# A two-layer decoder in split float32: token-major products in two of 256 columns, weights of theirs 128 bytes further on, other products gathered, and wide runs behind them

## The chip, the core and the metric

The kernel runs on one core of a Trainium2 chip. The metric is the device time of one execution in microseconds, as the median of the runs. In the profile PE is TensorE's matmul stream and PEld its weight loads, DVE is VectorE, ACT is ScalarE, POOL is GpSimd and SP is SyncE.

## What is computed

The input `x` has 256 tokens of 2,048 features. There are two layers. The first has a gated MLP that mixes tokens within chunks of 128, the second has attention with 16 heads and forget gates. Each ends with a feed-forward part (2,048 to 2 x 5,632, a causal convolution of width 3, SiLU gate, back to 2,048). The reference, cut to what matters:

```
def chunked_gmlp(xn, w_in, v_norm, w_s, b_s, w_out):
    z = gelu(xn @ w_in)
    u, v = split(z, 2)
    v = rmsnorm(v, v_norm)
    mixed = einsum('gts,bnsgc->bntgc', tril(w_s), v) + b_s
    return (u * mixed) @ w_out

def conv_ffn(xn, w_up, conv_w, conv_b, w_down):
    h = xn @ w_up
    h = sum(shift(h, k) * conv_w[k] for k in range(3)) + conv_b
    gate, val = split(h, 2)
    return (silu(gate) * val) @ w_down

h = x + chunked_gmlp(rmsnorm(x), ...)
h = h + conv_ffn(rmsnorm(h), ...)
k, v, c = keys, values, cumulative log forget gates of rmsnorm(h) @ w_kvf
h = h + forgetting_attention(rmsnorm(h), ..., k, v, c)
h = h + conv_ffn(rmsnorm(h), ...)
return rmsnorm(h)
```

All weights are float32, 418 MB of them are read once.

## The kernel before

**The products.** A float32 product is made of three in the type float32r. Each weight chunk is split into a rounded part `whi` (ACT, line 82) and the remainder `wlo` (DVE, line 83). The activations are kept as a rounded half and a remainder half side by side: `X1[:, kt, :256]` and `X1[:, kt, 256:]` (and `X2`, `H` in the same form). Needed are whi times both halves and wlo times the rounded half.

**The stream.** `Stream` (lines 40 to 102) runs a list of weight chunks of 128 x 1,024 numbers, 512 KB each, in order. At step i it loads chunk i + 6 (SP's queue), splits chunk i + 3 (ACT and DVE), multiplies chunk i (`mult`), and then advances every pending generator by one `yield`. The generators are what follows a block of chunks: evictions, norms, the convolution, the heads. So the instructions of such a step stand on every engine's queue behind the products of one chunk and ahead of those of the next. There are four buffers of each of `raw`, `whi` and `wlo`.

**Two orientations.** `feat_block` (line 168) makes two rows of 128 output features for all tokens: the weights are the stationary operand, the activations stream. A chunk has eight pieces of weights. Normally a piece of whi takes two products of 256 columns, one for each half of the activations, into the same 256 columns of the accumulator, and a piece of wlo takes one: 24 narrow products. Where the chunk's number is in `wide`, whi takes both halves in one product of 512 columns. Then the halves land side by side in the accumulator and have to be added afterwards (`both`, lines 309 to 316 and 323). `wide` is all four chunks for the first up block of a feed-forward part and for the gates `b_g`, the second chunk for the blocks of u, and the first chunk of some other blocks.

`tok_block` (line 214) makes 512 output features for two blocks of 128 tokens: the activations are loaded as the stationary operand, the weights stream, always 512 columns at a time, 12 products a chunk. It is used for v of the MLP, for q, k and v of the attention.

**Other products on TensorE.** They stand in generators between two chunks: mixing (line 489, one pair of groups behind each block of u), token sums and their transposes (350, 290), transposes of the normalised q and k (575, one for each token block), and for each head the scores (660, 661), the transposes of the probabilities (676) and the products with v (683 to 685), as three separate steps. These work on plain float32.

**Accumulators.** PSUM holds three double accumulators `ps` for the blocks (`main_ps`) and two single ones `mp` for the other products (`misc_ps`).

Of the kernel before, what the change touches and what calls it, by code (L numbers as in the profile page):

```python
# [17 lines left out]
P = 128  # L18
# [10 lines left out]
LOADS = 6  # L29
NEG = -3e38  # L30
# [9 lines left out]
class Stream:  # L40
# [7 lines left out]
    def chunk(self, src, mult, at_load=None, at_split=None):  # L48
        self.items.append((src, mult, at_load, at_split))

    def then(self, at_load=None, at_split=None, at_mult=None):
        self.items.append((None, at_mult, at_load, at_split))
# [9 lines left out]
    def _load(self, i):  # L62
        src, _, at_load, _ = self.items[i]
        if at_load:
            at_load()
        if src is None:
            return
        raw = self.pool.tile([P, CHUNK], F32, name="raw", tag="raw", bufs=LOADS - AHEAD + 1)
        raw = raw[:, :src.shape[1]]
        self.nc.sync.dma_start(raw, src)  # L70
        self.raw[i] = raw

    def _split(self, i):
# [6 lines left out]
        hi = self.pool.tile([P, CHUNK], F32R, name="whi", tag="whi")  # L80
        lo = self.pool.tile([P, CHUNK], F32R, name="wlo", tag="wlo")
# [51 lines left out]
def build(ctx, tc, d, out):  # L133
# [34 lines left out]
    def feat_block(src, x, K, done, wide=(), tiles=None):  # L168
# [6 lines left out]
        for c in range(n):  # L175
            def mult(hi, lo, c=c):
                if c == 0:
                    box["ps"] = tiles[0]() if tiles else main_ps()
                ps, xx = box["ps"], x()
# [3 lines left out]
                def product(part, half, j, m):  # L183
                    kt = 4 * c + j
                    w = part[:, j * 256 + m * P:j * 256 + (m + 1) * P]
                    first = kt == 0 and part is hi and half in (None, 0)
                    last = kt == K - 1 and part is lo
                    if half is None:
                        mm(ps[m], w, xx[:, kt, :], first, False)
                    else:  # L190
                        mm(ps[m][:, :T], w, xx[:, kt, half * T:(half + 1) * T], first, last)

                halves = (None,) if c in wide else (0, 1)
                if tiles and c == n - 1:
                    for m in range(2):
                        for j in range(4):
                            for half in halves:
                                product(hi, half, j, m)
                        for j in range(4):
                            product(lo, 0, j, m)  # L200
                        tiles[1](m, ps[m])
                else:
                    for j in range(4):
                        for m in range(2):
                            for half in halves:
                                product(hi, half, j, m)
                    for j in range(4):
                        for m in range(2):
                            product(lo, 0, j, m)
                if c == n - 1:  # L210
                    s.start(done(box["ps"], bool(wide)))
            s.chunk(src[c], mult)
# [4 lines left out]
    def tok_blocks(blocks, x, load=None, prep=None):  # L217
# [7 lines left out]
        for c, j0, nj in cuts:  # L225
            for i, ((src, done), box) in enumerate(zip(blocks, boxes)):
                def mult(hi, lo, c=c, j0=j0, nj=nj, done=done, box=box):
# [3 lines left out]
                    ps, xx = box["ps"], x()  # L231
                    for j in range(nj):
                        kt = kt0 + j
                        w = slice(j * 512, (j + 1) * 512)
# [16 lines left out]
                s.chunk(src[c][:, j0 * 512:(j0 + nj) * 512], mult,  # L251
# [26 lines left out]
    def token_sums():  # L278

        mp = misc_ps()  # L280
# [5 lines left out]
    def token_rows():  # L286

        mp = misc_ps()
# [44 lines left out]
    def last_tiles():  # L333

        tail["pairs"] = [main_ps() for _ in range(3)]
        tail["banks"] = [misc_ps() for _ in range(2)]
# [34 lines left out]
    def output():  # L371
# [3 lines left out]
        place = {(0, 0): pairs[1][:, 0, :], (1, 0): pairs[2][:, 0, :], (0, 1): pairs[1][:, 1, :],  # L375
                 (1, 1): pairs[2][:, 1, :], (0, 2): pairs[0][:, 0, :], (1, 2): pairs[0][:, 1, :],
                 (0, 3): banks[0], (1, 3): banks[1]}
# [78 lines left out]
    def v_done(blk):  # L456
        def done(ps):
            while not state["normed"]:
                yield
            _, vt, _, _, ss = mlp_kept()  # L460
            for tb in range(2):
                vv = vt[:, tb, blk * 512:(blk + 1) * 512]
                nc.scalar.activation(vv, ps[:, tb, :], AF.Gelu, scale=rcol[:, tb:tb + 1])
                sq = small.tile([P, 2, T], F32, name="sq", tag="sq", bufs=2)
                nc.scalar.activation(sq.rearrange("p a b -> p (a b)"), vv, AF.Square,
                                     accum_out=ss[:, tb, blk:blk + 1])
                yield
            if blk == 3:
# [5 lines left out]
                for tb in range(2):  # L474
                    nc.vector.tensor_scalar(vt[:, tb, :], vt[:, tb, :], rv[:, tb:tb + 1], None, op0=OP.mult)
        return done

    def u_done(p):
        def done(ps, both):
            X2, vt, wT, bB, _ = mlp_kept()  # L480
            u = ph.temp("u", [P, 2, T])
# [3 lines left out]
            mp = misc_ps()  # L485
            for m in range(2):
                g = 2 * p + m
                for n in range(2):
                    nc.tensor.matmul(mp[:, m * T + n * P:m * T + (n + 1) * P], vt[:, n, g * P:(g + 1) * P],  # L489
                                     wT[:, g, :], start=True, stop=True)  # L490
            mixed = ph.temp("mixed", [P, 2, T])
            for m in range(2):
                g = 2 * p + m
                nc.vector.scalar_tensor_tensor(
                    mixed[:, m, :].rearrange("p (n t) -> p n t", n=2),
                    mp[:, m * T:(m + 1) * T].rearrange("p (n t) -> p n t", n=2),
                    column(C_AVNORM + g), bB[:, g, None, :].to_broadcast([P, 2, P]), op0=OP.mult, op1=OP.add)
            nc.vector.tensor_tensor(u, u, mixed, op=OP.mult)
# [33 lines left out]
    def ffn(l, done):  # L532
        for i in range(KF):
            feat_block(d[f"up{l}"][4 * i:4 * i + 4], lambda: X1, KD, up_done(l, i),
                       range(4) if i == 0 else (0,) if i % 8 == 1 else ())
        for p in range(8):
            feat_block(d[f"down{l}"][11 * p:11 * p + 11], ffn_h, KF, done(p), (0,) if p % 4 == 0 else (),
# [16 lines left out]
    def head_norm(key, blk, gain):  # L554

        def done(ps):
            dst = att(key)
            for tb in range(2):
# [11 lines left out]
                                        r[:, :, None].to_broadcast([P, 4, P]), op=OP.mult)  # L570
                yield
                yield
# [5 lines left out]
                yield  # L578
        return done

    def v_evict(blk):
        def done(ps):
            v = att("v")
            for tb in range(2):
                nc.scalar.activation(v[:, tb, blk * 512:(blk + 1) * 512], ps[:, tb, :], AF.Copy,
                                     scale=rcol[:, tb:tb + 1])
            yield
            for hd in range(4 * blk, 4 * blk + 4):
                state["heads"].append(hd)
        return done  # L590

    def forget(hi, lo):
        X2 = att("X2")
        ps = main_ps()
        for kt in range(KD):
            w = slice(kt * NH, (kt + 1) * NH)
            if kt < KD - 1:
                mm(ps[:NH, 0, :], hi[:, w], X2[:, kt, :], kt == 0, False)
                mm(ps[:NH, 0, :T], lo[:, w], X2[:, kt, :T], False, False)
            else:  # L600
                mm(ps[:NH, 0, :T], lo[:, w], X2[:, kt, :T], False, False)
                mm(ps[:NH, 0, :], hi[:, w], X2[:, kt, :], False, True)
        s.start(forget_sums(ps))

    def forget_sums(ps):
# [3 lines left out]
        nc.scalar.activation(z, ps[:NH, 0, T:], AF.Copy)  # L609
        nc.vector.tensor_tensor(z, ps[:NH, 0, :T], z, op=OP.add)  # L610
# [29 lines left out]
        yield  # L640
        mp = misc_ps()
# [5 lines left out]
    def one_head(hd):  # L647
        q, k, v, ccol = att("q"), att("k"), att("v"), att("ccol")
        cB = ph.temp("cB", [P, T])
        nc.gpsimd.dma_start(cB, cd[hd:hd + 1, :].to_broadcast([P, T]))  # L650
        yield
        L = ph.temp("big", [P, 512], bufs=6)[:, :3 * P].rearrange("p (a b) -> p a b", a=3)
        mp = misc_ps()
        S = mp[:, :3 * P]
        nc.scalar.activation(L[:, 0, :], cB[:, :P], AF.Identity, scale=-1.0, bias=ccol[:, 0, hd:hd + 1])
        nc.scalar.activation(L[:, 1:, :], cB.rearrange("p (a b) -> p a b", a=2), AF.Identity, scale=-1.0,
                             bias=ccol[:, 1, hd:hd + 1])
        nc.gpsimd.affine_select(L[:, 0::2, :], L[:, 0::2, :], pattern=[[0, 2], [-1, P]], compare_op=OP.is_ge,
                                fill=NEG, base=0, channel_multiplier=1)
        nc.tensor.matmul(S[:, :P], q[:, hd, :P], k[:, hd, :P], start=True, stop=True)  # L660
        nc.tensor.matmul(S[:, P:], q[:, hd, P:], k[:, hd, :], start=True, stop=True)  # L661
        yield
        nc.vector.scalar_tensor_tensor(L, S.rearrange("p (a b) -> p a b", a=3), SCALE, L, op0=OP.mult, op1=OP.add)
        mx = ph.temp("mx", [P, 2])
        sm = ph.temp("sm", [P, 2])
# [151 lines left out]
```

## Time and profile before

| | |
|---|---|
| median of 3 runs | 2210.76 us (2210.67 to 2210.97) |
| the profiled execution, its own time | 2210.51 us |
| its span | 2208.8 us |
| granted TensorE clock | 0.999 |
| busy share of PE, DVE, ACT | 100%, 66%, 52% |
| HBM read | 417.88 MB |

The span is the time from the first to the last instruction on the core; the execution's own time adds what lies around it. Rows of groups read: line, engine, operation, output and inputs, size of the stationary operand (128*128), size of the moving one, count, then busy time, mean length of one in ns, and idle time before. Matmuls overlap in the records: a length of 276 ns stands for a product that is followed by the next one after 113. So a pace is read from starts, or from a stretch with a count.

### The profile page before, as it was taken

The numbers are of one execution on the slowest core, as the hardware profiler recorded it, in microseconds if no ns is written. First come the engines' busy times: TensorE is split into PE (matmuls) and PEld (weight loads), VectorE is DVE, ScalarE is ACT, GpSimd is POOL, SyncE is SP. The second block draws the span as 40 slices with busy tenths as digits, with TensorE's granted clock in tenths as the row PEclk, the third lists the DMA queues.
The fourth block names the chain that finished last, engine by engine and source line by source line (L and its number), as shares of the span: only waits on it lengthen the run. The fifth ranks groups of instructions, "written<-read, shape, count | busy, mean of one in ns | idle before, by whom it ended". The sixth has DMA issues, their size and how long they took to land.

```text
span 2208.8 us, 41643 instructions
## 1 busy us (share of the span) xinstructions
PE 2199.4 (100%) x17208; PEld 2105.5 (95%) x17208; DVE 1465.0 (66%) x2107; ACT 1154.1 (52%) x1549; POOL 19.0 (1%) x41
## 2 busy tenths in 40 slices
PE   9999999999999999999999999999999999999998
PEld 7899999999999999998788888999999999999998
DVE  6676677777777755557786566667777777765553
ACT  5545455555555544345444666556555555544443
POOL 0000000000000000000000110000000000000000
PEclk9999999999999999999999999999999999999999
DMA  8555565556555655665565555656556565655653
GB/s 304 178 192 178 195 196 196 192 194 197 192 191 195 197 191 184 207 192 172 174 186 185 173 163 184 195 189 195 191 194 196 187 198 194 198 192 194 195 192 134
DMA packets 116910, 422.70 MB, mean 191 GB/s; under 512 B 13280, under 2 KB 13680, under 8 KB 116464
## 3 DMA queue, kind: packets, MB, share of 16 engines
q1 hardware_dynamic: 115776, 417.93, 57.8%
q8 instruction: 134, 2.20, 0.4%
q0 software_dynamic: 768, 2.10, 0.4%
q14 instruction: 56, 0.46, 0.1%
q10 hardware_dynamic: 176, 0.02, 0.0%
HBM read 417.88 MB, written 2.11 MB: 190 GB/s over the span
## 4 chain that ended last, share of the span: by engine, by line
PE 99%; DMA 0%; DVE 0%; ACT 0%; ACTq 0%; issue 0%; SPq 0%; DVEq 0%
PE ps L166 96%; PE mp L166 1%; DMA raw<-a_in_v 0%; PE mp L489 0%; PE mp L575 0%; PE mp L661 0%; PE mp L676 0%; PE mp L685 0%; PE mp L684 0%; PE mp L660 0%; PE mp L683 0%; PE mp L350 0%; DVE h L402 0%; DVE wlo L83 0%; ACT whi L82 0%; ACTq L811 0%
## 5 line engine op out<-in xcount | busy, mean ns | idle before, releaser
L83 DVE TENSOR_TENSOR wlo<-raw,whi 128x1024 fp32r<-128x1024 f32 (+1 forms) x787 | 954.8, 1219 | 461.1 <-ACT whi L82 459.3
L82 ACT ACTIVATE whi<-raw 128x1024 fp32r<-128x1024 f32 (+1 forms) x787 | 826.8, 1056 | 670.9 <-PE ps L166 602.4
L166 PE MATMUL ps<-X,whi 128*128 128x256 f32 (+1 forms) x6176 | 827.8, 286 | 0.0
L166 PEld LDWEIGHTS ps<-X,whi 128*128 128x128 f32 x6176 | 758.3, 188 | 16.5
L166 PE MATMUL ps<-X,wlo 128*128 128x256 f32 x3328 | 445.5, 276 | 0.0
L166 PEld LDWEIGHTS ps<-X,wlo 128*128 128x128 f32 x3328 | 413.2, 188 | 5.5
L166 PE MATMUL ps<-ffn_H,whi 128*128 128x256 f32 (+1 forms) x2696 | 342.9, 277 | 0.0
L166 PEld LDWEIGHTS ps<-ffn_H,whi 128*128 128x128 f32 x2696 | 322.7, 188 | 1.1
L166 PE MATMUL ps<-ffn_H,wlo 128*128 128x256 f32 x1364 | 186.6, 276 | 0.0
L166 PEld LDWEIGHTS ps<-ffn_H,wlo 128*128 128x128 f32 x1364 | 170.2, 188 | 0.4
L166 PE MATMUL ps<-whi,att_X 128*128 128x512 f32 x512 | 168.1, 400 | 0.0
L523 DVE SCALAR_TENSOR_TENSOR ffn_c<-ffn_a,col,ffn_c 128x255 f32<-128x255 f32 x352 | 162.0, 481 | 6.3
L166 PE MATMUL ps<-whi,X 128*128 128x512 f32 x512 | 161.6, 395 | 0.5 <-ACT whi L82 0.5
L519 ACT ACTIVATE ffn_c<-ffn_a,col 128x256 f32<-128x256 f32 x176 | 96.4, 595 | 49.8 <-DVE ffn_a L316 49.8
L166 PEld LDWEIGHTS ps<-whi,X 128*128 128x128 f32 x512 | 96.0, 188 | 21.9 <-ACT whi L82 1.2
L166 PEld LDWEIGHTS ps<-whi,att_X 128*128 128x128 f32 x512 | 96.2, 188 | 20.4
L316 DVE TENSOR_TENSOR ffn_a<-ps,rB 128x512 f32<-128x512 f32 x74 | 51.2, 692 | 96.7 <-PE ps L166 96.7
L166 PE MATMUL ps<-wlo,X 128*128 128x512 f32 x256 | 99.4, 391 | 0.8 <-DVE wlo L83 0.8
L166 PE MATMUL ps<-wlo,att_X 128*128 128x512 f32 x256 | 100.0, 390 | 0.0
L258 ACT ACTIVATE X<-h,col 128x256 fp32r<-128x256 f32 x64 | 29.1, 501 | 84.4 <-DVE h L322 67.8
L166 PE MATMUL ps<-att_X,whi 128*128 128x256 f32 (+2 forms) x520 | 68.9, 281 | 0.0
L166 PEld LDWEIGHTS ps<-att_X,whi 128*128 128x128 f32 (+1 forms) x520 | 61.5, 185 | 2.2
(160 smaller groups left out, 1156.3 us busy)
## 6 DMA issues: line engine op xcount, KB each, us to landing
raw<-up SPq DMA_DIRECT2D x352, 512.0 KB, 3.4
raw<-down SPq DMA_DIRECT2D x176, 512.0 KB, 4.1
raw<-a_in_u SPq DMA_DIRECT2D x32, 512.0 KB, 3.9
raw<-a_out SPq DMA_DIRECT2D x32, 512.0 KB, 4.2
raw<-b_q SPq DMA_DIRECT2D x32, 512.0 KB, 4.2
raw<-kvf_k SPq DMA_DIRECT2D x32, 512.0 KB, 4.2
raw<-kvf_v SPq DMA_DIRECT2D x32, 512.0 KB, 4.0
raw<-b_g SPq DMA_DIRECT2D x32, 512.0 KB, 3.3
```

The source lines that it names most:

```text
L82: self.nc.scalar.activation(hi[:, :n], raw, AF.Copy)
L83: self.nc.vector.tensor_tensor(lo[:, :n], raw, hi[:, :n].bitcast(F32), op=OP.subtract)
L166: nc.tensor.matmul(o, a, b, start=start, stop=stop, skip_group_check=True)
L258: nc.scalar.activation(dst[:, kt, :T], h[:, kt, :], AF.Copy, scale=g)
L316: nc.vector.tensor_tensor(a, src, rB[:, None, :].to_broadcast([P, 2, T]), op=OP.mult)
L519: nc.scalar.activation(c[:, m, :], a[:, m, :], AF.Identity, scale=w[2], bias=column(C_CONVB + l * 2 * KF + f))
L523: nc.vector.scalar_tensor_tensor(c[:, m, n:], a[:, m, :T - n], w[k], c[:, m, n:], op0=OP.mult, op1=OP.add)
```

## The change

**Narrow token-major products.** `tok_blocks` takes 256 columns of weights at a time, so each former product becomes two with the same stationary operand, except where a wide run is due.

**Where the weights lie.** Each buffer of `whi` and `wlo` gets 64 more columns (`PAD`), 4,352 bytes a partition instead of 4,096. Feature-major chunks are split into its beginning, token-major ones 32 columns (128 bytes) further on.

**Wide runs by position.** The argument `wide` of `feat_block` goes. `between()` sets a list `[8, 2]`: the next chunk makes its first eight products with 512 columns, the chunk after it its first two, and then all is narrow. It is called ahead of every group of other products, at the change from token-major to feature-major, and behind four blocks in each up stage (i = 1, 12, 23, 34). The kernel begins with `[12] * 8 + [8, 2]`.

**Gathering.** Mixing is made in two groups of 16 products into four `mp` (`mixing`), kept in SBUF, and the blocks of u pick it up. The transposes of q and k for both token blocks stand together. `heads` is one generator of 18 steps: in each step the products with v of head n - 2, the transposes of head n - 1 and the scores of head n stand together, one step every three chunks.

**Accumulators.** Two `ps`, four `mp`. The first two blocks of v are copied out of PSUM before their scale is known (`v_done`). The gates wait for their own two heads instead of all.

The core of the diff:

```
+PAD = 64
+FEAT_AT, TOK_AT = 0, 32
...
-        hi = self.pool.tile([P, CHUNK], F32R, name="whi", tag="whi")
-        lo = self.pool.tile([P, CHUNK], F32R, name="wlo", tag="wlo")
+        at = self.items[i][4]
+        hi, lo = (self.pool.tile([P, CHUNK + PAD], F32R, name=k, tag=k)[:, at:at + CHUNK] for k in ("whi", "wlo"))
...
-        return psum.tile([P, 2, 512], F32, name="ps", tag="ps", bufs=3)
+        return psum.tile([P, 2, 512], F32, name="ps", tag="ps", bufs=2)
...
-        return psum.tile([P, 512], F32, name="mp", tag="mp", bufs=2)
+        return psum.tile([P, 512], F32, name="mp", tag="mp", bufs=4)
...
+    def between():
+        state["wide"] = [8, 2]
+
+    def wide_next():
+        return state["wide"].pop(0) if state["wide"] else 0
...
+                ps, xx, wide = box["ps"], x(), wide_next()
+                box["both"] |= wide > 0
...
+                def rounded(j, m):
+                    nonlocal wide
+                    w = hi[:, j * 256 + m * P:j * 256 + (m + 1) * P]
                     kt = 4 * c + j
+                    if wide > 0:
+                        mm(ps[m], w, xx[:, kt, :], kt == 0, False)
+                        wide -= 1
                     else:
+                        for half in range(2):
+                            mm(ps[m][:, :T], w, xx[:, kt, half * T:(half + 1) * T], kt == 0 and half == 0, False)
...
+                    left = wide_next()
...
                         def product(tb, lower, part):
+                            nonlocal left
                             at = lower * T + tb * P
-                            mm(ps[:, tb, :], xx[:, kt, at:at + P], part[:, w],
-                               kt == 0 and part is hi and not lower, kt == KD - 1 and lower == 1)
+                            n, left = 512 if left > 0 else 256, left - 1
+                            for i in range(0, 512, n):
+                                mm(ps[:, tb, i:i + n], xx[:, kt, at:at + P], part[:, j * 512 + i:j * 512 + i + n],
+                                   kt == 0 and i == 0 and part is hi and not lower, kt == KD - 1 and lower == 1)
...
+            if not state["normed"]:
+                for tb in range(2):
+                    nc.scalar.activation(vv[tb], src[tb], AF.Copy)
+                src = vv
...
-            feat_block(d[f"up{l}"][4 * i:4 * i + 4], lambda: X1, KD, up_done(l, i),
-                       range(4) if i == 0 else (0,) if i % 8 == 1 else ())
+            feat_block(d[f"up{l}"][4 * i:4 * i + 4], lambda: X1, KD, up_done(l, i))
+            if i % 11 == 1:
+                s.then(at_mult=between)
...
-            while state["done"] < NH or state["gates"] < p:
+            while state["done"] < 2 * p + 2 or state["gates"] < p:
...
-        feat_block(d["b_g"][4 * p:4 * p + 4], lambda: X1, KD, g_done(p), range(4))
+        feat_block(d["b_g"][4 * p:4 * p + 4], lambda: X1, KD, g_done(p))
```

The order on TensorE at two places, before and after. The first is the q stage, token-major, where the first block of q is normalised and transposed (`ident` streams, `att_big` is loaded; `X_73` is X1). Before:

```order
L166 MATMUL ps<-whi,X_73 128x512
L575 MATMUL mp<-ident,att_big 128x128 x4
L166 MATMUL ps<-whi,X_73 128x512
L166 MATMUL ps<-wlo,X_73 128x512
L166 MATMUL ps<-whi,X_73 128x512 x2
L166 MATMUL ps<-wlo,X_73 128x512
```

After:

```order
L168 MATMUL ps<-whi,X_73 128x256 x2
L615 MATMUL mp<-ident,att_big 128x128 x8
L168 MATMUL ps<-whi,X_73 128x512
L168 MATMUL ps<-wlo,X_73 128x512
L168 MATMUL ps<-whi,X_73 128x512 x2
L168 MATMUL ps<-wlo,X_73 128x512
L168 MATMUL ps<-whi,X_73 128x512 x2
L168 MATMUL ps<-wlo,X_73 128x512
L168 MATMUL ps<-whi,X_73 128x256 x4
L168 MATMUL ps<-wlo,X_73 128x256 x2
L168 MATMUL ps<-whi,X_73 128x256 x2
L168 MATMUL ps<-whi,X_73 128x512
```

Eight transposes stand together where there were two times four; behind them come eight wide products, eight narrow ones to the end of the chunk, and the last row is the first of the two wide ones of the next chunk.

The second place is the gates `b_g`, feature-major, among the heads (`att_pT` with `att_v` are the products with v, `att_k` with `att_q` the scores). Before:

```order
L683 MATMUL mp<-att_pT,att_v 128x128
L684 MATMUL mp<-att_pT,att_v 128x128
L685 MATMUL mp<-att_pT,att_v 128x128
L660 MATMUL mp<-att_k,att_q 128x128
L661 MATMUL mp<-att_k,att_q 128x256
L166 MATMUL ps<-X_73,whi 128x512 x8
L166 MATMUL ps<-X_73,wlo 128x256 x8
L676 MATMUL mp<-ident,att_big 128x128 x3
L166 MATMUL ps<-X_73,whi 128x512 x8
L166 MATMUL ps<-X_73,wlo 128x256 x8
```

After:

```order
L720 MATMUL mp<-att_pT,att_v 128x128
L725 MATMUL mp<-ident,att_big 128x128 x3
L728 MATMUL mp<-att_k,att_q 128x128
L729 MATMUL mp<-att_k,att_q 128x256
L168 MATMUL ps<-X_73,whi 128x512 x8
L168 MATMUL ps<-X_73,wlo 128x256 x8
L168 MATMUL ps<-X_73,whi 128x512 x2
L168 MATMUL ps<-X_73,whi 128x256 x12
L168 MATMUL ps<-X_73,wlo 128x256 x8
L168 MATMUL ps<-X_73,whi 128x256 x16
L168 MATMUL ps<-X_73,wlo 128x256 x8
L718 MATMUL mp<-att_pT,att_v 128x128
```

Every chunk had a gap and eight wide products; now one chunk in three has eight, the next one two, the third none, and the transposes have moved between the products with v and the scores.

More of the change, by code (lines that the diff above doesn't have):

```diff
@@ L196, in mult @@
                         for j in range(4):
-                            for half in halves:
-                                product(hi, half, j, m)
+                            rounded(j, m)
                         for j in range(4):
-                            product(lo, 0, j, m)
+                            remainder(j, m)
                         tiles[1](m, ps[m])
                 else:
[L203 to L209, printed above, removed]
+                    for product in (rounded, remainder):
+                        for j in range(4):
+                            for m in range(2):
+                                product(j, m)
                 if c == n - 1:
-                    s.start(done(box["ps"], bool(wide)))
-            s.chunk(src[c], mult)
+                    s.start(done(box["ps"], box["both"]))
+            s.chunk(src[c], mult, FEAT_AT)
     def tok_block(src, x, done):
@@ L278, in token_sums @@
     def token_sums():
+        between()
         mp = misc_ps()
@@ L286, in token_rows @@
     def token_rows():
+        between()
         mp = misc_ps()
@@ L333, in last_tiles @@
     def last_tiles():
-        tail["pairs"] = [main_ps() for _ in range(3)]
-        tail["banks"] = [misc_ps() for _ in range(2)]
+        tail["pairs"] = [main_ps() for _ in range(2)]
+        tail["banks"] = [misc_ps() for _ in range(4)]
         return tail["pairs"][0][:, 0, :], tail["banks"][0]
@@ L484, in done @@
             nc.scalar.activation(u, u, AF.Gelu)
[L485 to L498, printed above, removed]
+            while state["mixed"] < 2 * p + 2:
+                yield
+            nc.vector.tensor_tensor(u, u, ph.keep("mixed", [P, NH, T])[:, 2 * p:2 * p + 2, :], op=OP.mult)
             yield
@@ L570, in done @@
                                         r[:, :, None].to_broadcast([P, 4, P]), op=OP.mult)
+                normed.append(n)
                 yield
-                yield
+            yield
+            between()
+            for tb, n in enumerate(normed):
                 mp = misc_ps()
@@ L586, in done @@
                                      scale=rcol[:, tb:tb + 1])
+            state["v"] += 4
             yield
-            for hd in range(4 * blk, 4 * blk + 4):
-                state["heads"].append(hd)
         return done
@@ L640, in forget_sums @@
         yield
+        between()
         mp = misc_ps()
@@ L715, in build @@
     tail = {}
-    state = {"normed": False, "layer": 0, "heads": [], "done": 0, "gates": 0}
+    state = {"normed": False, "layer": 0, "mixed": 0, "v": 0, "done": 0, "gates": 0, "wide": [12] * 8 + [8, 2]}
     cd = dram.tile([NH, T], F32, name="cd")
```

203 lines of the change are left out of this document (119 added, 84 removed).

## Prediction

> **What bounds the kernel now.** I read the page first: busy time by engine, then the chain that ended last.
>
> ```profile
> span 2208.8 us, 41643 instructions
> PE 2199.4 (100%) x17208; PEld 2105.5 (95%) x17208; DVE 1465.0 (66%) x2107; ACT 1154.1 (52%) x1549; POOL 19.0 (1%) x41
> ...
> PE 99%; DMA 0%; DVE 0%; ACT 0%; ACTq 0%; issue 0%; SPq 0%; DVEq 0%
> ```
>
> TensorE is never free: 99% of the chain is its own instructions. DVE and ACT have a third and a half of the span left. So only what changes the pace of TensorE's products counts, and the kernel has two kinds of them. The groups by shape give their numbers ("whi,X" with 512 columns: the activations are loaded as the stationary operand and the weights stream, token-major; "X,whi": the weights are loaded, feature-major):
>
> ```profile
> L166 PE MATMUL ps<-whi,att_X 128*128 128x512 f32 x512 | 168.1, 400 | 0.0
> L166 PE MATMUL ps<-whi,X 128*128 128x512 f32 x512 | 161.6, 395 | 0.5 <-ACT whi L82 0.5
> L166 PE MATMUL ps<-X,whi 128*128 128x512 f32 x480 | 124.3, 401 | 0.0
> L166 PE MATMUL ps<-wlo,att_X 128*128 128x512 f32 x256 | 100.0, 390 | 0.0
> L166 PE MATMUL ps<-wlo,X 128*128 128x512 f32 x256 | 99.4, 391 | 0.8 <-DVE wlo L83 0.8
> L166 PE MATMUL ps<-ffn_H,whi 128*128 128x512 f32 x32 | 8.1, 395 | 0.0
> L166 PE MATMUL ps<-mlp_X,whi 128*128 128x512 f32 x8 | 2.1, 404 | 0.0
> L166 PE MATMUL ps<-att_X,whi 128*128 128x512 f32 x8 | 2.0, 395 | 0.0
> ```
>
> The first, second, fourth and fifth row are the token-major products, 1,536 in all, every one "wide" (512 columns). The other four are wide products of feature-major chunks: 480 + 32 + 8 + 8 = 528, 66 chunks of eight. All other feature-major products are "narrow" (256 columns). Mean durations overlap and don't add, so the pace has to come from stretches. The busy time by stretch, cut at starts of products:
>
> ```profile
> 20.04:58.50 38.46, 38.46 (x170) 31.55 (x168) 1.00 0.85 311
> 292.22:373.82 81.60, 81.60 (x722) 81.60 (x721) 1.00 0.60 194
> 1343.59:1387.96 44.37, 44.37 (x258) 38.66 (x257) 1.00 0.60 189
> ```
>
> The third column of numbers counts weight loads, one for each product; the granted clock behind it is 1.00. The first stretch is token-major, 14 chunks of 12 wide products: 38.46 / 168 = 228.9 ns each. The second is feature-major and all narrow, 30 chunks of 24 (one load reaches in from before): 81.60 / 720 = 113.3 ns, so a pair takes 226.7 ns. The third is 16 feature-major chunks with eight wide and eight narrow products: 44.37 / 16 = 2.773 us, where an all-narrow chunk takes 24 x 113.3 = 2.720 us. A chunk with eight wide ones is 0.053 us dearer, or 6.6 ns for each.
>
> The last view is the sequence on TensorE among the attention heads, where feature-major narrow products show a second pace:
>
> ```profile
> 1300.32 0.39 PE L166 MATMUL ps<-X,whi 128*128 128x512 f32 x1
> 1300.55 1.11 PE L166 MATMUL ps<-X,wlo 128*128 128x256 f32 x8
> 1301.49 0.49 PE L676 MATMUL mp<-ident,att_big 128*128 128x128 f32 x3
> 1301.74 2.11 PE L166 MATMUL ps<-X,whi 128*128 128x512 f32 x8
> ...
> 1303.45 0.40 PE L166 MATMUL ps<-X,whi 128*128 128x512 f32 x1
> 1303.69 1.08 PE L166 MATMUL ps<-X,wlo 128*128 128x256 f32 x8
> 1304.60 0.38 PE L683 MATMUL mp<-att_pT,att_v 128*128 128x128 f32 x2
> ```
>
> Columns: start, length, then the group. From 1300.55 eight narrow products take 0.94 us, 117.5 ns each; from 1303.69 eight take 0.91. The slow eight have products of 1.11 us in all against 1.08, and they don't recover within the eight. They come behind an eight-wide run whose last member was the short one (0.39 us); the fast eight behind one whose last was the long one (0.40). So a run of products of another kind (softmax and mixing products, transposes) can leave narrow products in a slow pace, 4.2 ns dearer each, and a wide run of eight clears it only sometimes. In before, nothing narrow ever follows such products without a wide run, and the token-major stages have no narrow products at all.
>
> **The change part by part.**
>
> *Token-major products in two of 256.* Of 1,536, 298 stay wide (72 in the first chunks, the rest in the runs behind other products), 1,238 become 2,476 narrow ones with as many loads. The trace has no narrow token-major product. Its nearest rows are the feature-major narrow ones, at 113.3 ns in 81.60 us. The 128-byte shift makes the two alike. In the built program X begins at byte 36,192 of a partition and the first weight tile at 87,968, which is 96 and 160 modulo 256: loaded weights lie 64 ahead of the streamed X. With the streamed weights at 160 + 128 = 288, 32 modulo 256, the loaded X at 96 lies 64 ahead too, and all steps in the tiles are multiples of 256 bytes. So I take 113.3: 1,238 x (228.9 - 226.7) = 2.8 us less. The bounds are that and 117.5 ns from the slow eight, which would be 1,238 x (235.0 - 228.9) = 7.6 us more. The 298 left wide are moved to the feature-major position, so between 228.9 ns (nothing) and the feature-major 226.7 + 6.6 = 233.3 (1.3 us more); I take the latter. Sum: -1.5 us.
>
> The Trainium skill, page "TensorE: Matmul & The Clock Gate", section "Back-to-back issue gap", speaks against splitting: a product of N columns takes N / 2.4 + 2.5 ns, so 109.2 for 256 and 215.8 for 512, and a pair costs 2.5 ns more than a wide one. By that the split would cost 1,238 x 2.5 = 3.1 us, an estimate from that page. The trace differs: 226.7 for a pair and 228.9 to 233.3 for a wide one.
>
> *Feature-major wide products.* 528 become 238: runs of eight and two behind other products, and one such pair of runs in every eleven up blocks. Before: 66 x 0.053 = 3.5 us. After: 238 x 6.6 ns = 1.6. Sum: -1.9 us.
>
> *Slow eights.* Before has six among the heads; these are the first and the last:
>
> ```profile
> 1293.31 1.11 PE L166 MATMUL ps<-X,wlo 128*128 128x256 f32 x8
> ...
> 1329.51 1.11 PE L166 MATMUL ps<-X,wlo 128*128 128x256 f32 x8
> ```
>
> They all follow a gather that ends with the two products of the scores (L660, L661). After has 16 gathers that end so, each followed by eight wide and eight narrow products, in token-major chunks too. At 0.94 - 0.907 = 0.033 us each: 16 x 0.033 - 6 x 0.033 = +0.35 us. Then the run of two comes. Whether it ends the slow pace no row shows, since in before an interruption always comes first. If it doesn't, 20 narrow products of that chunk and 24 of the next stay slow: 16 x 44 x 4.2 ns = 3.0 us more. The other bound is that no eight is slow, -0.2. I take +0.35, because in before the wide run that follows a slow eight comes out fast (1301.74 to 1303.69).
>
> *Gathering.* In the programs' order, runs of other products on TensorE go from 67 to 36 (mixing 8 to 2, normalised q and k 16 to 8, heads three a head to one). What a run costs beyond its own products is small:
>
> ```profile
> 1025.01 0.40 PE L166 MATMUL ps<-whi,X 128*128 128x512 f32 x1
> 1025.24 0.60 PE L575 MATMUL mp<-ident,att_big 128*128 128x128 f32 x4
> 1025.60 0.48 PE L166 MATMUL ps<-whi,X 128*128 128x512 f32 x1
> 1025.92 0.40 PE L166 MATMUL ps<-wlo,X 128*128 128x512 f32 x1
> ```
>
> From 1025.24 to 1025.92 there are four transposes and one wide product: 0.68 - 0.229 = 0.451, 0.113 each, the pace of a narrow product. What is the run's own is no more than the rounding of these starts, 0.02. 31 runs fewer: between 0 and -0.6 us; I take -0.3.
>
> *What costs nothing, and its cover.* Main accumulators go from three to two, so a block waits for the eviction of the one before the last. Evictions take 0.68 us for each half, as v's do here; a chunk takes 2.7:
>
> ```profile
> L585 ACT ACTIVATE att_v<-ps,rcol 128x512 f32<-128x512 f32 x8 | 5.0, 680 | 1.7 <-PE ps L166 1.7
> ACT whi L82 <- PE ps L166: 602.4, 423, 2.2
> ```
>
> The tightest place is the first blocks, worked two at a time: the third needs the first one's accumulator one chunk after it ends. The new copy of it (two of 0.68) ends 1.4 us before that. ACT is not behind there: its splits wait for TensorE (602.4 us, 423 times), three chunks ahead. Behind the copies on ACT stands only the next split, which has that lead. Without the cover it would cost 1.4 us once. The heads' steps keep three chunks from scores to transposes; The blocks without wide products lose their extra addition on ACT and DVE. SP's loads keep their order; on POOL the fetch of a head's row now stands behind the mask of the head before, three chunks ahead of its use.
>
> Sum: -1.5 - 1.9 + 0.35 - 0.3 = **-3.4 us**. The profiled execution took 2210.51 us (span 2208.8), 0.25 below the median of 2210.76, so the median becomes **2207.4** and the span about 2205.4. With each cost at its better end it is -2.8 - 1.9 - 0.2 - 0.6 = -5.5 (2205.3), at the worse end of all but the token-major pace -1.5 - 1.9 + 3.35 = 0.0 (2210.8).
>
> **The rivals.**
>
> *A, the better ends* (token-major wide products keep 228.9 ns, slow eights vanish, gathers save their 0.02 each): about 2205.5. For it: the token-major rows are cheaper than the feature-major ones today. Against: the new position is the feature-major one. 0.20.
>
> *B, slower: the slow pace takes the token-major stages.* All 2,476 new narrow products run at 117.5 ns: 2,476 x 4.2 = 10.4 us more, 2217.8. For it: narrow products there are new, follow about two thirds of the gathers, and the slow pace is stable for eight products. Against: the feature-major rows return to 113.3 after almost every run. It decides from (3.4 + 4.4) / 4.2 ns = 1,860 slow products on, three quarters of them; at 810 the gain is gone. 0.12.
>
> *C, slower: the weight tiles' spacing.* With the 256 bytes of padding, four buffers no longer lie 4,096 bytes apart but 4,352, so the distance to X alternates by 256 bytes from chunk to chunk, in feature-major chunks too. If that mattered, half of some 15,000 narrow products would be slow: 7,500 x 4.2 = 31 us, 2239. For it: no row has that distance. Against: distances that differ by 512 (the two halves of a weight tile) show one pace. 0.05.
>
> *D, a fixed cost in each product*, so that two narrow ones cost more than a wide one. Priced as the mirror of the 2.2 ns that a feature-major pair gains on a token-major wide product: (1,238 + 290) x 2.2 ns = +3.4, with +0.35 and -0.3 about 2214.2. Against: every narrow stretch of the trace. 0.03. The Trainium skill's formula ("TensorE: Matmul & The Clock Gate", "Back-to-back issue gap") gives much the same, 1,528 x 2.5 ns = 3.8 us in place of 3.4, an estimate from that page.
>
> That the change doesn't do what it says can be left out: the order shows the runs of eight and two behind each gather.
>
> **How the numbers follow.** The measurement can tell about 0.2% (4.4 us) from no change. The forecast has 0.60 and lies within that, at -0.15%; D lies within it too: same 0.63. A is just beyond on the fast side: faster 0.20. B and C: slower 0.17. The range leaves out B, C and D (0.20) and holds the forecast and A: 2205.0 to 2211.0.
>
> **What would show it.** Token-major stretches at 113.3 ns a narrow product (B: 117.5); feature-major chunks of 2.72 us in all four buffers (C: two of four near 24 x 117.5 = 2.82); after a gather that ends in scores, eight slow products, then, behind the two wide ones, 113.3 again; no idle time of TensorE at the third block, some 50 us in. A TensorE that waits anywhere, or token-major pairs above 229 ns, would make the prediction wrong.

## The result, and the profile after

| | before | after |
|---|---|---|
| median | 2210.74 us (2210.67 to 2210.97) | 2226.19 us (2225.93 to 2227.21) |
| the profiled execution, its own time | 2210.51 us | 2226.11 us |
| its span | 2208.8 us | 2224.4 us |

The changed kernel is slower: ratio 1.0071, 95% interval 1.0053 to 1.0088. The forecast was 2207.4, its range ended at 2211.0.

The page of the changed kernel, the same three rows as of before:

```profile
span 2224.4 us, 44685 instructions
...
PE 2199.7 (99%) x18736; PEld 2168.3 (97%) x18736; DVE 1454.5 (65%) x2092; ACT 1163.2 (52%) x1550; POOL 21.2 (1%) x41
...
PE 92%; DVE 4%; ACT 2%; issue 1%; DMA 0%; ACTq 0%; SPq 0%; DVEq 0%
```

TensorE's busy time has hardly grown (2199.4 to 2199.7). What has changed is the chain: DVE and ACT now hold 6% of it, where they held none. (That share counts the work behind each wait as well, so it is larger than the waits themselves.) Before, TensorE's list of waits had, beside the wait for `ident` at the start, two rows:

```profile
PE ps L166 <- DVE wlo L83: 0.8, 1, 0.8
PE ps L166 <- ACT whi L82: 0.5, 1, 0.5
```

After (total us, times, longest us):

```profile
PE mp L615 <- DVE att_big L606: 9.8, 7, 1.8
PE mp L725 <- DVE att_big L751: 3.8, 5, 1.5
PE mp L367 <- DVE acc L324: 1.7, 1, 1.7
...
PE ps L168 <- DVE wlo L85: 1.2, 2, 0.8
```

That is 16.5 us against 1.3: 15.2 us of new waits, in three places. The first are the transposes of q and k (L615), the second the heads (L725), the last two lie around the third block of v (of the 1.2 us for wlo, 0.8 are at the kernel's start, as before).

The time has grown by 15.6 us, but the forecast had it shrink by 3.4, so 18.8 us have to be explained. The rest, some 3.5 us, hides in the busy time: TensorE is busy for 2199.7 us here and for 2196.2 in experiment 5 below, which has almost no waits. A wait is counted only from the modelled end of the product ahead of it, so a stop costs a little more than the wait that is listed. Experiment 5, at its first transposes of q:

```profile
1030.12 1.03 PE L620 MATMUL mp<-ident,att_big 128*128 128x128 f32 x8
1031.22 0.40 PE L168 MATMUL ps<-wlo,X 128*128 128x512 f32 x1
```

From the first transpose to the second product behind the transposes it takes 1.10 us. In the changed kernel the same stretch takes 2.79 (1030.01 to 1032.80 in the rows under "Why TensorE waits" below): 1.69 more, where 1.45 are listed. At five of the seven stops at L615 the difference comes to 0.20 to 0.25 us, which for the 15 stops of the list makes 3.0 to 3.8 us, an estimate.

The pace, on which the sum was built, is as forecast. A narrow token-major stretch of k and a narrow feature-major stretch of the first up stage, cut at starts of products:

```profile
1109.78:1131.09 21.31, 21.31 (x189) 1.00 0.58 182
305.71:422.22 116.51, 116.51 (x1030) 1.00 0.65 199
```

The counts hold a product or two that reach in; 188 and 1,028 start there: 113.4 and 113.3 ns. And behind a gather among the gates, the slow eight and what follows the run of two:

```profile
1306.82 2.22 PE L168 MATMUL ps<-X,whi 128*128 128x512 f32 x8
1308.88 1.10 PE L168 MATMUL ps<-X,wlo 128*128 128x256 f32 x8
1309.83 2.00 PE L168 MATMUL ps<-X,whi 128*128 128x512 f32 x14
1311.66 1.07 PE L168 MATMUL ps<-X,wlo 128*128 128x256 f32 x8
1312.57 0.62 PE L168 MATMUL ps<-X,whi 128*128 128x256 f32 x4
```

Eight narrow products take 0.95 us from 1308.88, then come two wide and twelve narrow ones, and the next eight take 0.91: the run of two ends the slow pace.

**Why TensorE waits at q and k.** Selected rows of DVE, ACT and PE behind the first block of q, whose last product ends at 1022.0:

```profile
1022.05 0.69 ACT L598 ACTIVATE sq<-ps,rcol 128x512 f32<-128x512 f32 x1 [1.26 <-PE ps L168]
1022.77 0.69 DVE L601 TENSOR_REDUCE att_hv<-sq 128x4 f32<-128x512 f32 x1 [0.73 <-ACT sq L598]
1026.02 0.69 DVE L606 TENSOR_TENSOR att_big<-ps,att_hr 128x512 f32<-128x512 f32 x1
1026.62 1.22 DVE L85 TENSOR_TENSOR wlo<-raw,whi 128x1024 fp32r<-128x1024 f32 x1
1026.74 0.69 ACT L598 ACTIVATE sq<-ps,rcol 128x512 f32<-128x512 f32 x1 [2.66 <-DVE att_big L606]
1028.15 0.68 DVE L601 TENSOR_REDUCE att_hv<-sq 128x4 f32<-128x512 f32 x1
1030.01 0.60 PE L615 MATMUL mp<-ident,att_big 128*128 128x128 f32 x4
1031.32 0.69 DVE L606 TENSOR_TENSOR att_big<-ps,att_hr 128x512 f32<-128x512 f32 x1
1032.06 0.66 PE L615 MATMUL mp<-ident,att_big 128*128 128x128 f32 x4 [1.45 <-DVE att_big L606]
1032.80 0.40 PE L168 MATMUL ps<-wlo,X 128*128 128x512 f32 x1
```

The chain of one block of tokens, from the reduce to the end of the normalise, is 3.9 us (1022.77 to 1026.71). The second block's square on ACT starts only behind the first block's normalise (ACT waits 2.66 us for it), and its chain runs from 1028.15 to 1032.01. From the first square to the end of the second normalise it takes 10.0 us. The transposes of both stand three chunks behind the block, at 1030.01, which leaves 8.0. The second four start at 1032.06. Before, at the same place:

```profile
1019.94 0.69 ACT L561 ACTIVATE sq<-ps,rcol 128x512 f32<-128x512 f32 x1 [1.29 <-PE ps L166]
1027.82 0.68 ACT L561 ACTIVATE sq<-ps,rcol 128x512 f32<-128x512 f32 x1
1033.94 0.60 PE L575 MATMUL mp<-ident,att_big 128*128 128x128 f32 x4
```

There the second block's square, and with it its transposes, came three chunks after those of the first (1025.24 and 1033.94), so the same two chains had 14.0 us. The change left two steps between the second normalise and its transposes, as before; it moved the second chain two steps closer to the first.

**At the start**, the copies of the first two blocks of v:

```profile
48.54 1.09 ACT L479 ACTIVATE mlp_vt<-ps 128x512 f32<-128x512 f32 x2 [7.10 <-PE ps L168]
49.52 1.06 ACT L84 ACTIVATE whi<-raw 128x1024 fp32r<-128x1024 f32 x1
...
52.47 2.97 ACT L84 ACTIVATE whi<-raw 128x1024 fp32r<-128x1024 f32 x3
```

ACT stands 7.10 us in front of the first copy, waiting for the last product of the first block, with the splits of the third block behind it. The two `s.then` items between the blocks carry no chunk; in the stream they take the places of two chunks, so the split "three chunks ahead" is here one chunk ahead.

**Among the gates**, ACT loads its tables:

```profile
L764 ACT ACT_TABLE_LOAD x4 | 5.1, 1283 | 0.0
L746 ACT ACT_TABLE_LOAD x3 | 3.8, 1283 | 6.4 <-DVE att_mx L745 6.4
```

L746 is the heads' exponential, L764 the gates' sigmoid. Since a gate now waits for its own two heads only, the two functions alternate: seven loads of 1.283 us at these two lines, where experiment 3 below leaves one. Those ahead of L746 stand inside a head's chain: each starts only when ACT has waited some 2.1 us for DVE's maximum (6.4 us in three), so it is not hidden in that wait.

### The profile page after: what moved, and what is told of

Same layout as the page of the kernel before. It is cut to its first block, busy times and chain, and to the rows that moved or that the text cites. A ratio compares the mean times of both kernels' runs of the same rounds, so it can differ in the third digit from the quotient of the medians.

```text
span 2224.4 us, 44685 instructions
## 1 busy us (share of the span) xinstructions
PE 2199.7 (99%) x18736; PEld 2168.3 (97%) x18736; DVE 1454.5 (65%) x2092; ACT 1163.2 (52%) x1550; POOL 21.2 (1%) x41
## 4 chain that ended last, share of the span: by engine, by line
PE 92%; DVE 4%; ACT 2%; issue 1%; DMA 0%; ACTq 0%; SPq 0%; DVEq 0%
PE ps L168 90%; DVE wlo L85 1%; PE mp L168 1%; ACT whi L84 1%; DVE att_hv L601 0%; DMA raw<-a_in_v 0%; DVE rs_t L290 0%; DVE rs_t L289 0%; DVE att_hr L291 0%; PE mp L512 0%; PE mp L725 0%; ACT sq L598 0%; PE mp L729 0%; PE mp L615 0%; DVE att_big L606 0%
## 5 line engine op out<-in xcount | busy, mean ns | idle before, releaser
L168 PEld LDWEIGHTS ps<-X,whi 128*128 128x128 f32 x6418 | 773.2, 188 | 8.8
L168 PE MATMUL ps<-ffn_H,whi 128*128 128x256 f32 x2728 | 342.7, 276 | 0.0
L168 PE MATMUL ps<-whi,att_X 128*128 128x256 f32 (+1 forms) x935 | 163.3, 290 | 0.0
L168 PE MATMUL ps<-whi,X 128*128 128x256 f32 (+1 forms) x929 | 160.6, 290 | 0.0
L168 PEld LDWEIGHTS ps<-whi,att_X 128*128 128x128 f32 x935 | 131.0, 188 | 5.6
L168 PEld LDWEIGHTS ps<-whi,X 128*128 128x128 f32 x929 | 129.7, 188 | 5.2 <-ACT whi L84 0.3
L168 PE MATMUL ps<-wlo,X 128*128 128x256 f32 (+1 forms) x457 | 99.8, 291 | 1.2 <-DVE wlo L85 1.2
L168 PE MATMUL ps<-wlo,att_X 128*128 128x256 f32 (+1 forms) x453 | 100.0, 292 | 0.0
L168 PEld LDWEIGHTS ps<-wlo,X 128*128 128x128 f32 x457 | 71.0, 188 | 3.6 <-DVE wlo L85 1.7
L168 PEld LDWEIGHTS ps<-wlo,att_X 128*128 128x128 f32 x453 | 70.4, 188 | 1.6
```

What stands on the lines that cost most here:

```text
L168: nc.tensor.matmul(o, a, b, start=start, stop=stop, skip_group_check=True)
```

## The experiments

All times are medians. The kernel before took 2210.65 to 2210.85 us beside them.

**1. One more step at q and k** (the changed kernel otherwise).

```
                 normed.append(n)
                 yield
             yield
+            yield
             between()
```

> One more step (a chunk, 2.7 us) between the normalise of q and k and their transposes; everything else is the changed kernel. Theory: the 1.2 to 2.0 us that TensorE waits between the fourth and the fifth transpose, 9.8 us in seven waits for DVE plus about 2 us around them, are a lack of distance only: DVE's two chains of 4 us do not fit in the 8 us to the third chunk. With the step they vanish: 2226.2 - 12 = 2214 us, and no row of TensorE waiting for DVE att_big at the transposes. Rival (gathering itself or the pace behind it costs the time): the waits may go, but the time stays within 2 us of 2226.

2218.60 us (2216.29 to 2219.83): 7.6 less, not 12. The waits at the transposes are gone from the list, but a longer one now stands at its head, at the transposes of the heads:

```profile
PE mp L726 <- DVE att_big L752: 5.5, 5, 2.4
```

The wait for the first head has grown from 0.6 to 2.4 us: the last block of k, pushed back a chunk, now stands on DVE ahead of its softmax. The place is the right one; the distance was taken from the next stage. The profiled run (2219.28) also holds two stretches at half the granted clock, which experiment 4 and the last section come back to.

**2. The start.**

```
-    s.then(at_load=lambda: nc.sync.dma_start(col[:, C_KVNORM:], d["col"][:, C_KVNORM:]))
-    s.then(at_load=load_mix)
+    third = len(s.items)
     for block in v_blocks[2:]:
         tok_blocks([block], lambda: X1)
+    s.items[third] = s.items[third][:2] + (rest_and_mix,) + s.items[third][3:]
```

(`rest_and_mix` issues the same loads.)

> The two empty items of the stream behind the first two blocks of v go; their loads are issued with the first chunk of the third block instead. Theory: the empty items eat two of the three chunks of lead, so that the splits of the third block stand on ACT behind the new copies; with the lead back TensorE waits for neither wlo nor the token sums: 2.7 us less, 2223.5. Rival (the copies themselves load ACT and DVE too much at that place): the waits stay, 2226.

2224.05 us (2223.95 to 2224.13): 2.1 less. The waits for wlo go from 1.2 to 0.8 us, that of the token sums from 1.7 to 0.4. So the copies cost next to nothing with three chunks of lead, and the lost lead was the price. Most of it was paid at the token sums, not at the splits.

**3. The gates wait for all heads.**

```
-            gg = ph.temp("big", [P, 512], bufs=6).rearrange("p (a b) -> p a b", a=2)
+            gg = att("k")[:, 2 * p:2 * p + 2, :]
...
-            while state["done"] < 2 * p + 2 or state["gates"] < p:
+            while state["done"] < NH or state["gates"] < p:
```

> The gates wait for all heads again, as in the kernel before, and keep their values in the rows of k that no head needs any more. Theory: the waits of TensorE for the normalised probabilities among the gates come from ACT loading its table anew (1.28 us each) when sigmoid stands between exponentials; 6 of the 12 table loads go and with them some 4 us: 2222. Rival (the chain of a head is too long for three feature-major chunks anyway): the table loads go, the waits stay, 2226.

2222.85 us (2221.87 to 2223.39): 3.3 less.

```profile
L764 ACT ACT_TABLE_LOAD x1 | 1.3, 1283 | 0.0
```

```profile
PE mp L725 <- DVE att_big L751: 0.6, 1, 0.6
```

Of the waits among the heads only the first head's is left. (The profiled run has a stretch at half the granted clock near its start, so 3.3 may be a little low.) The rule of the Trainium skill, "ScalarE: Activation LUTs", section "Rules for kernel authors" (do all functions of one table set before switching), bears on exactly this edit; the switch that it budgets at about 2.7 us took 1.283 us here, with no more than 0.02 us between the load and the instruction behind it.

**4. The three together.**

> The three edits together. Theory: all of the difference to the forecast is waits of TensorE for chains on DVE and ACT, and the terms of pace were right: 2226.2 - 12 - 2.7 - 4 = 2207.5, about 3 us under the kernel before. Rival: the waits make up only part, and narrow token-major products or gathers lose time that the kernel before does not lose: 2210.7 or above.

2210.00 us (2209.63 to 2213.68), 16.2 less, and a spread of 4 us. The profiled run (2211.51) has a stretch that explains part of the spread. TensorE's wait for the first head, then the windows around and behind it (the number behind the count is the granted clock):

```profile
1202.77 0.87 PE L730 MATMUL mp<-ident,att_big 128*128 128x128 f32 x3 [2.40 <-DVE att_big L756]
```

```profile
1200.50:1202.50 2.00, 0.00 (x0) 1.00 0.42 170
1203.00:1206.00 3.00, 3.00 (x10) 0.50 0.84 202
1206.50:1209.50 3.00, 3.00 (x22) 1.00 0.87 274
```

Behind the wait the clock is granted at 0.50 for 3.4 us (from 1202.7 to 1206.1), and then at 1.00 again. At half the clock that is some 1.7 us on top of the 2.4. The mean clocks of the eleven runs fit: it is 0.998 in four of the five above 2211 us, and 0.999 in the fifth and in the six below.

**5. The heads begin two chunks later** (with the three edits).

```
         fetch(0)
+        yield
+        yield
         yield
```

> The three edits, and the heads begin two chunks later. Theory: with the longer spacing the last block of k stood on DVE ahead of the softmax of head 0 and TensorE waited 2.4 us once, behind which its clock was granted at 0.50 for 3.6 us (1.8 us more). Both go: 2210.0 - 4.2 = 2205.8 us, all single runs within 1 us of each other, 0.2% under the kernel before. Rival: the wait only moves to the next place where DVE is full (the first block of v, the gates): 2210.

2207.76 us (2207.37 to 2209.10), 2.2 under the median of experiment 4 and 4.1 under its profiled run (2207.38 against 2211.51). Against the kernel before: ratio 0.9987, interval 0.9978 to 0.9996. This version is faster than both kernels, if by little against the one before.

```profile
span 2205.7 us, 44679 instructions
...
PE 2196.2 (100%) x18736; PEld 2167.3 (98%) x18736; DVE 1454.5 (66%) x2093; ACT 1152.8 (52%) x1545; POOL 21.7 (1%) x41
```

```profile
PE ps L168 <- DVE wlo L85: 1.0, 2, 0.8
PE mp L367 <- DVE acc L324: 0.4, 1, 0.4
```

The waits are down to 1.4 us, where the kernel before has 1.3. Experiments 6 to 10 start from this kernel.

**6. Token-major weights not shifted.**

```
-FEAT_AT, TOK_AT = 0, 32
+FEAT_AT, TOK_AT = 0, 0
```

> The kernel with all four edits, but token-major weights at the beginning of their buffers as the feature-major ones (no shift by 128 bytes). Theory of the forecast (the place of the loaded operand against the streamed one sets the pace): the narrow token-major products, 2,476 of them, fall to a pace of 116.7 to 117.8 ns: 2,476 x 3.4 to 4.4 = 8 to 11 us more, about 2215. Rival (the place is of no matter): no difference, 2206.

2214.64 us (2212.89 to 2215.69): 6.9 more. A narrow token-major stretch of k:

```profile
1109.62:1131.76 22.14, 22.14 (x189) 22.13 (x188) 17.23 (x44) 9.30 (x10) 0.00 (x0) 1.00 0.52 155
```

22.14 / 188 = 117.8 ns. The runs of eight and two stand where they stood, but at this place they mostly don't bring the fast pace back: of the 2,432 products in the trace's token-major stretches of eight or more narrow ones, 2,092 go at some 117.8 ns and 340 at some 113.4. In experiment 5 only 24 go at 117.8. So the place of the weights against the loaded X decides, in most stretches, whether they do.

**7. Token-major products wide again.**

```
-                            n, left = 512 if left > 0 else 256, left - 1
+                            n = 512
```

> The kernel with all four edits, but all token-major products with 512 columns again, at the shifted place. Theory: 1,238 pairs of 226.7 ns become wide products of 228.9 to 233.3 ns (the shifted place is that of the feature-major wide ones): 2.8 to 8.2 us more, 2208.6 to 2214. Rival (splitting saves nothing): 2206.

2215.12 us (2214.83 to 2215.85): 7.4 more. A stretch of q:

```profile
1050.03:1055.86 5.83, 5.83 (x26) 4.67 (x25) 5.38 (x17) 4.41 (x6) 0.00 (x0) 1.00 0.26 90
```

5.83 / 25 = 233.2 ns, not the 228.9 of before: at the shifted place a token-major wide product costs what a feature-major one does, the dearer of the two values that the forecast weighed.

**8. No wide runs behind other products.**

```
-        state["wide"] = [8, 2]
+        state["wide"] = []
```

> The kernel with all four edits, but no wide runs behind other products (those at the kernel's beginning stay). Theory: narrow products behind an interruption stay in the slow pace of 117.8 ns until something ends it: some 100 chunks of u, q, k, v and the gates, 24 products each, 4.4 ns each, 10 us, less the 166 wide products there at 6.6 ns, 1.1 us: 2206 + 9 = 2215. Rival (the pace comes back by itself within a few products): 2205.

2273.23 us (2269.84 to 2278.56): 65 more, where 9 were expected. A stretch of the first up stage:

```profile
300.00:400.00 100.00, 100.00 (x851) 100.00 (x850) 70.35 (x99) 53.04 (x72) 0.00 (x0) 1.00 0.64 192
```

100 / 850 = 117.6 ns. The expectation counted only chunks near gathers; in fact the slow pace, once there, holds through both feed-forward parts, where no other products and no wide ones come between. In the trace these are two stretches of 6,288 and 6,240 products at 117.8 ns each: 4.5 ns too much for each makes 56 of the 65 us, and the rest lies in the token-major stages and among the heads. Not every gather leaves the slow pace: behind the second run of mixing products 1,344 narrow ones take 113.4 ns each with no wide run at all.

**9. The run of eight alone.**

```
-        state["wide"] = [8, 2]
+        state["wide"] = [8]
```

> The kernel with all four edits, but behind other products only the run of eight wide products, without the run of two a chunk later. In the trace of the kernel with the four edits 10 of some 50 runs of eight leave the slow pace behind them, and the run of two ends it each time. Theory: without it those stretches stay slow to the next run; among them are the one from the mixing (300 products) and the two behind the token sums, and whether one of the eight long stretches of the feed-forward parts (1,028 products, 4.5 us each) or of the two in front of the next stage (some 3,000, 13 us each) falls slow is by chance: 2209 to 2235. Rival (the slow pace ends by itself, the two are not needed): 2207.5.

2213.26 us (2210.44 to 2217.26): five of the ten runs lie at 2210.4 to 2211.6, the others at 2214.9 to 2217.3. In the profiled run (2211.62), a slow eight among the gates stays slow to the next gather:

```profile
1299.87 1.10 PE L168 MATMUL ps<-X,wlo 128*128 128x256 f32 x8
...
1302.69 1.10 PE L168 MATMUL ps<-X,wlo 128*128 128x256 f32 x8
1303.64 2.05 PE L168 MATMUL ps<-X,whi 128*128 128x256 f32 x16
1305.52 1.11 PE L168 MATMUL ps<-X,wlo 128*128 128x256 f32 x8
1306.47 0.38 PE L725 MATMUL mp<-att_pT,att_v 128*128 128x128 f32 x2
```

From 1302.69 to 1306.47 there are 32 products, 118 ns each. The two groups of runs would fit a long stretch that falls slow in one and not in the other (1,040 products without the run of two, 4.7 us); no trace of a run of the upper group was taken, so that stays argued.

**10. Transposes of q and k apart for each block of tokens**, as before (the transposes move into the loop over `tb`, two steps behind the normalise, with a `between()` each).

> The kernel with all four edits, but the transposes of q and k stand apart for each block of tokens, as in the kernel before (16 places of four instead of 8 of eight, a wide run behind each). Theory: distance was the whole fault of that place, gathering itself is worth only the wide runs and the edges that it spares: 8 x (10 x 6.6 ns + 0.02) = 0.7 us more, 2208.5, and no wait at the transposes. Rival (gathering is where the gain is): 2211 or above.

2208.36 us (2207.79 to 2209.35): 0.6 more than gathered, as expected, and no wait at the transposes. The single runs of the two overlap (2207.37 to 2209.10 gathered), so gathering these transposes is worth at most what it spares in wide runs.

**11. One chain for both blocks of tokens** (the changed kernel, distance unchanged).

```
+            for tb in range(2):
+                nc.scalar.activation(sqs[tb], ps[:, tb, :], AF.Square, scale=rcol[:, tb:tb + 1])
...
+            rsqrt(r, v, 8)
...
```

> The changed kernel with no more distance at q and k, but one chain on DVE for both blocks of tokens: both squares first on ACT, one row of small operations for eight values instead of two for four. Theory: what was missing there is the time of two chains of 4 us and of ACT's second square that stood behind the first; one chain takes about 4 x 0.69 + 14 x 0.2 = 5.6 us and ends some 2 us before the transposes: their waits go at the same distance, 11.2 us less, and the heads, not pushed together, keep no wait of 2.4 us: 2215. Rival (two gathered transposes wait for something other than DVE's chain): unchanged, 2226.

2215.47 us (2214.58 to 2216.63): 10.7 less, 0.5 beside the expected. The waits at the transposes are gone at the old distance, so what TensorE waited for was the length of two chains, one behind the other. How much the earlier square gives and how much the shared small operations, this run does not separate. Some is given back at the splits (1.2 us of waits in the changed kernel), probably because DVE is now held for a whole chain at once:

```profile
PE mp L731 <- DVE att_big L757: 3.1, 4, 1.5
PE ps L168 <- DVE wlo L85: 2.3, 3, 1.1
```

**12. One chain, start and gates together**, with the heads where the changed kernel has them.

> The one chain together with the edits of the start and of the gates; the heads begin where the changed kernel has them. Theory: no wait of TensorE beyond those of the kernel before is left: 2207.6, as with the four edits. Rival (the first head still meets the last block of k on DVE): 2209 to 2211 with a wide spread.

2208.46 us (2207.90 to 2208.96), ratio to the kernel before 0.9990 (0.9981 to 0.9999): 0.9 above the expected, with 1.8 us of waits for wlo where experiment 5 has 1.0, and without the wide spread of the rival. Two ways of mending the schedule (experiments 5 and 12) come out within 1.1 us of the forecast's 2207.4.

## Why the prediction was wrong, point by point

- **The failed step is "What costs nothing, and its cover".** It named covers for three moved steps, took "three chunks ahead" from the list of the stream and "three chunks from scores to transposes" from the list of yields, and measured neither against the length of the chains that have to fit in. The kernel lost 15.2 us of listed waits there, and some 3 us around them. The prediction had named a TensorE that waits anywhere as a sign of being wrong, and that sign came.
- *The transposes of q and k* had no cover named at all: they appear only as a saving, under "Gathering". Two squares and two chains of 3.9 us took 10.0 us where the gathered transposes leave 8.0; before, they had 14.0. The chain of before could have been read from its trace (1019.94 to 1033.94 above). Price 10.7 us (experiment 11).
- *The heads' three chunks* are enough for the chain as it was; the chain became longer by table loads that the edit of the gates brings. The diff in "The change" has that edit, and the prediction has no term for it. Price 3.3 us (experiment 3).
- *The third block of v.* "Which has that lead" was false where the stream has items without chunks. The estimate that missing cover would cost 1.4 us once has the right size, 2.1 us (experiment 2), but partly by luck: 1.3 of the 1.7 us of waits that went were at the token sums, which it did not name.
- The three prices add to 16.1 us. Experiments 5 and 12 lie 18.4 and 17.7 under the changed kernel; the remaining 2 us or so are not assigned to a place.
- **The pace terms held, but for a small one.** With the waits out, the kernel takes 2207.76 us, 3.1 under before, and TensorE's busy time is 3.2 under before (2196.2 against 2199.4); the forecast had 3.4. Narrow token-major products run at 113.4 ns where 113.3 was taken, the wide ones at the shifted place at 233.2 where 233.3 was. The term for slow eights was wrong: it had one behind each of the 16 gathers that end in scores. In experiment 5's trace only one of these 16 leaves one, and of all 46 runs of eight, 8 do. Before has eight too, since two behind its token sums (at 285.49 and 1485.68) come on top of the six counted. So the term was about nothing instead of +0.35, and where the run of two follows, it ends the slow pace each time. In "Gathering", the heads of before have about two runs each and not three; the difference of 31 runs is right.
- **The rivals.** B, the slow pace in the token-major stages, did not come, but its mechanism is real: it comes without the shift (experiment 6) or without the runs (8). C did not come: the long stretches, which go through all four buffers, run at 113.3. D did not: a pair of narrow products is cheaper than any wide one. A's condition failed with the 233.2 ns of experiment 7. None of the rivals was a wait for DVE or ACT, the one mechanism that came.

## What to carry to other kernels

When a step is gathered or moved in a kernel whose first engine is never free, write down for each the time from its input to its use, and the summed length of everything that stands on the other engines' queues in that time; a count of chunks or yields is not a time. An empty item in a pipelined list takes lead from its neighbours, and a wait relaxed for one engine can make two functions alternate on another. Repair by moving distance only after looking at which stage it is taken from (experiments 1 and 4).

## What the runs showed of the hardware that was not expected

- A TensorE that stands 2.4 us can be given half its clock for 3.4 us after (experiments 1 and 4, at the first head). In the profiled runs of experiments 1 and 3 an idle time of 1.7 us at the token sums did the same (granted 0.50 from 66.2 to 69.7 and from 65.4 to 68.8), while in the profiles of the changed kernel and of experiment 11 the same idle time did not. Experiment 1, then the changed kernel, behind that idle time:

```profile
66.50:67.00 0.50, 0.50 (x3) 0.40 (x2) 0.40 (x4) 0.00 (x0) 0.00 (x0) 0.50 1.05 123
66.50:67.00 0.50, 0.50 (x4) 0.41 (x3) 0.40 (x3) 0.00 (x0) 0.00 (x0) 1.00 1.15 123
```

  The Trainium skill, "TensorE: Matmul & The Clock Gate", section "HAM oscillation — how this bites in real kernels", warns of idle gaps over about 3.4 us; here shorter ones were enough, some of the time.
- The slow pace of narrow products, 117.6 to 117.8 ns, did not end by itself in two steady streams of 740 and 735 us (experiment 8), and the few hundred wide products in the runs of eight and two are worth 65 us in this kernel.
- Whether those wide products help depended on where the streamed and the loaded operand lie against each other: 128 bytes are worth 6.9 us (experiment 6). Why, no run here shows.
